# Order of the chunk pairs in one unit: pairs 0 to 7 in natural order, seven-product pairs at places 3, 5, 6 and 7

## The chip, the cores and the metric

The kernel runs on one core of one Trainium2 chip. The metric is device time in microseconds (us). Three runs of the kernel before gave a median of 2133.9 us (2133.49 to 2135.06). Engines are named as the profile names them: PE is TensorE (matmuls), PEld its weight loads, DVE is VectorE, ACT is ScalarE, POOL is GpSimd, and SP is SyncE, which here only issues DMAs.

## What is computed

The reference is one decoder layer on 16 meta tokens and 256 tokens, model width 2048, in float32: a feed-forward block, a mixer of attention and a short convolution, and a second feed-forward block. The change touches the second feed-forward block only:

```python
def swiglu_ffn(h, w_gu, w_down):
    gate, up = jnp.split(h @ w_gu, 2, axis=-1)
    return (jax.nn.silu(gate) * up) @ w_down

    s = s + merged @ w_out[layer]
    h = rms_norm(s, norm_ffn2[layer])
    s = s + 0.5 * swiglu_ffn(h, ffn2_w_gu[layer], ffn2_w_down[layer])
```

## The kernel before

**Precision.** Each float32 operand is split into a high part (a cast by ACT, `wh`, line 531) and a low part (a subtraction by DVE, `wl`, line 532). A product is three matmuls into one PSUM bank: high by high, low by high, high by low (lines 644 to 646).

**Units.** Feed-forward two has 5632 hidden columns, taken in eleven units of 512 columns of gate and 512 of up. A unit (`gate_up_mix`, line 763, through `mixed` and `linear_mix`) multiplies 256 tokens (two blocks of 128) by eight pairs of 128-row chunks of the weights. So each pair is a 2 x 2 block product, and it is done in one of three forms, which the plan of the unit gives by letter:

- D: eight products, straightforward, into banks 2, 3, 4 and x. Two weight tiles of two columns each.
- P: seven products, with sums of blocks in the place of blocks, into banks 1 to 7. Four weight tiles, the first with one column. The sums of the weight blocks were prepared earlier and lie in DRAM (`made`, list `MADE`, lines 74 and 75); they are loaded as `t24` and `t13` (lines 673 and 674). The sums of the activation blocks (`a.sums`) are computed in the kernel.
- S: as P, with the weight sums made on the spot by DVE. The first unit has none.

All pairs of a unit add up in the same eight banks. `left` (line 635) counts the products that each bank still lacks, and when a bank is complete, `done` in `mixed` evicts it. Bank x is fed by D pairs only, and its eviction is a copy by ACT to `u2x` (line 736). The pool has eight banks (line 88) for everything, transposes included.

**Order.** The plan of the first unit is `FFN2_FIRST` (line 49). Its first entry gives the form at each of the eight places, its last the pair that stands at each place: pairs 0, 1, 3, 4, 5, 2, 6, 7 as D, D, P, D, P, D, P, P. The other units have no such entry and take the pairs in order. `linear_mix` reads the list at line 632 and uses it for the weight loads (lines 666, 673, 674), the activation blocks (line 704) and their sums (line 711). Loads are called two places ahead (`far`); weight tiles are made up to three tiles ahead of their products (`step`, line 299, `AHEAD`). Buffers: three for `st`, two for `t24` (tag "tt"), four each for `wh` and `wl`.

**The activations of the first unit.** They come from the stage just before, the output projection `w_out` (`add_mix` with OUT_FIRST and OUT, lines 1263 and 1264), whose results lie token by token in `sT`. For each pair, `turned` (line 1174) transposes four blocks on PE into a bank (`h_ps`, line 1180) and splits them into high (`h`, ACT, line 1184) and low (DVE, line 1185). `sum_of_parts` (line 579) and `combine` (line 586) then make the block sums of a pair for P: one addition (`mf`, line 583), four short operations (`sums`, lines 589 to 592), and a split (`sp`, lines 614 and 615). `mf` and `sums` come from the tag "sc" with two buffers, the same two in which the one-column `wh` and `wl` of each P place are made (line 521).

Pairs 0 to 3 are transposed during the last part of the output projection, with the sums of pairs 2 and 3. For pairs 4 to 7, `out_done(1)` (line 1248) puts six jobs on the list `side`, and each place of the first unit takes one when its last product has been issued (line 660): the transposes of pair 4 at place 0, of pair 5 with its sum at place 1, of pair 6 with its sum at place 2, of pair 7 at place 3, the sum of pair 7 at place 4, and the norm (`norm_tok`) at place 5.

**Queues.** Each engine works off its queue in order. The order of a queue is fixed when the program is built, from the program's order and from when operands and buffers are expected to be free; so an instruction whose buffer isn't free can stand behind later ones.

Of the kernel before, what the change touches and what calls it, by code (L numbers as in the profile page):

```python
# [15 lines left out]
P = 128  # L16
# [4 lines left out]
F = 5632  # L21
DC = D // P
GC = 4
GW = GC * P
# [21 lines left out]
GATES = ("PSDSDSDS", (), {(0, 3): 1, (2, 1): 3, (4, 1): 5, (6, 1): 7}, ())  # L46
Q = ("DSDSDSDS", (), {(0, 1): 1, (2, 1): 3, (4, 1): 5, (6, 1): 7}, ())
B_PLAN = ("DSDSDSDS", (2, 4), {(0, 1): 1, (2, 1): 3, (4, 1): 5, (6, 1): 7}, ())
FFN2_FIRST = ("DDPDPDPP", (1,), {}, (), (0, 1, 3, 4, 5, 2, 6, 7))
FFN2 = ("DDPPDSPP", (1,), {(4, 1): 5}, ())  # L50
FFN2_MORE = ("DPPPDSPP", (2,), {(4, 1): 5}, ())
OUT_FIRST = ("DDSDSDSD", (1,), {(1, 1): 2, (3, 1): 4, (5, 1): 6}, ())
# [9 lines left out]
MORE_IN = (4, 5, 6, 7, 8, 9, 10)  # L62


def _made_in(plan):
    return [plan[4][i] if plan[4:] else i for i, kind in enumerate(plan[0]) if kind == "P"]


def _unit_plan(u):
    return FFN2_MORE if u in MORE_IN else FFN2 if u else FFN2_FIRST  # L70


GATE_UNITS = [GATES_FIRST] + [GATES] * (D // GW - 1)
MADE = [(0, d, p) for d, plan in enumerate(GATE_UNITS) for p in _made_in(plan)]
MADE += [(1, u, p) for u in range(F // GW) for p in _made_in(_unit_plan(u))]


@with_exitstack
def decoder_layer(ctx: ExitStack, tc: tile.TileContext, t, out):
    nc = tc.nc  # L80
# [9 lines left out]
    def bank(name):  # L90
        return psum.tile([P, 512], F32, tag="acc", name=name)
# [41 lines left out]
    def load_vectors():  # L133
# [7 lines left out]
        out=mask[:, T - P :],  # L141
        in_=mask[:, T - P :],
# [156 lines left out]
    def step(use, ring=True):  # L299

        ahead.append((use, ring))
        while sum(r for _, r in ahead) > AHEAD:
            ahead.pop(0)[0]()
# [10 lines left out]
    made = [[{} for _ in range(n // GW)] for n in (D, F)]  # L314
# [25 lines left out]

    for n, (f, u, p) in enumerate(MADE):
        spare.extend(Making(n, made[f][u], p, k) for k in range(2))
# [98 lines left out]
    def flush():  # L441
        while pending:
            pending.pop(0)()
# [74 lines left out]
    def parts(src, n=2, held=False):  # L518

        wh, wl = (  # L520
            tmp.tile([P, 1, GW], F32R, tag="sc", name=nm) if n == 1
            else (held_tile(nm) if held else wpool.tile([P, 2, GW], F32R, tag=nm, name=nm))
            for nm in ("wh", "wl")
        )
        wh, wl = wh[:, :n, :], wl[:, :n, :]
        with ExitStack() as order:
            if n == 1 and part_last:

                for ins in part_last:
                    order.enter_context(tc.issue_after(ins))  # L530
            part_last[:] = [nc.scalar.copy(out=wh, in_=src).ins]  # L531
            part_last.append(nc.vector.tensor_sub(wl, src, wh.bitcast(F32)).ins)  # L532
        return wh, wl
# [88 lines left out]
    def linear_mix(plan, a, w, name, done, k0=0, made=None, pairwise=False):  # L622

        kinds, turn_at, sums_at, by_load = plan[:4]
        at = plan[4] if plan[4:] else range(len(kinds))
        nd = kinds.count("D")
        ns = len(kinds) - nd
        left = {k: 2 * nd * (k in "234x") + ns * (k != "x") for k in "1234567x"}
        ps = {}

        def product(k, left_op, wh, wl):
            first = k not in ps
            if first:  # L640
                ps[k] = bank(name + k)
            left[k] -= 1
            hi, lo = left_op
            nc.tensor.matmul(ps[k], hi, wh, start=first, stop=False)  # L644
            nc.tensor.matmul(ps[k], lo, wh, start=False, stop=False)  # L645
            nc.tensor.matmul(ps[k], hi, wl, start=False, stop=left[k] == 0)  # L646
            if left[k] == 0:
                done(k, ps[k])

        def use(p, n, products):  # L650

            for k, left_op, wh, wl in products:
                product(k, left_op, wh, wl)
            if p in turn_at and later:
                later.pop(0)()
            if n == (1 if kinds[p] == "D" else 3):
                if p == 0:
                    flush()
                if side:
                    side.pop(0)()  # L660

        def load(p):

            st = wpool.tile([P, 4, GW], F32, tag="st", bufs=ST_BUFS, name="st")
            n = 3 if p in by_load or kinds[p] == "P" else 4
            nc.sync.dma_start(out=st[:, :n, :], in_=w[k0 // 2 + at[p], :, :n, :])
            if kinds[p] == "P":
                if pairwise:
                    t13s[p] = wpool.tile([P, 2, GW], F32, tag="tt", bufs=2, name="t13")
                else:  # L670
                    t13s[p] = aux.tile([P, 2, GW], F32, tag="act", name="t13")
                t24s[p] = wpool.tile([P, 2, GW], F32, tag="tt", bufs=2, name="t24")
                nc.sync.dma_start(out=t24s[p], in_=made[at[p]][:, 2:4, :])
                nc.sync.dma_start(out=t13s[p], in_=made[at[p]][:, 0:2, :])
            if kinds[p] == "S":
                if not by_load and (made is None or pairwise):
                    t13s[p] = wpool.tile([P, 2, GW], F32, tag="tt", bufs=2, name="t13")
                elif p not in by_load:
                    t13s[p] = aux.tile([P, 2, GW], F32, tag="act", name="t13")
                t24s[p] = wpool.tile([P, 2, GW], F32, tag="tt", bufs=2, name="t24")  # L680
            return st

        def sums(k):
            st, t13, t24 = loaded[k], t13s[k], t24s[k]
            if k not in by_load:
                nc.vector.tensor_add(t13, st[:, 1:3, :], st[:, 3:4, :].to_broadcast([P, 2, GW]))
            nc.vector.tensor_add(t24[:, 0, :], t13[:, 0, :], st[:, 2, :])
            last_sum[:] = [nc.vector.tensor_add(t24[:, 1, :], t24[:, 0, :], st[:, 0, :]).ins]  # L688

        t13s, t24s = {}, {}  # L690

        def prefetch(p):
            t13 = t13s[p] = aux.tile([P, 2, GW], F32, tag="act", name="t13")
            nc.gpsimd.dma_start(out=t13, in_=w[k0 // 2 + p, :, 1:3, :])
            nc.gpsimd.dma_start(out=t13, in_=w[k0 // 2 + p, :, 3:5, :], accum_op=ALU.add)

        far = 2 if by_load or (made is not None and not pairwise) else 1
        loaded = {k: load(k) for k in range(far)}
        for p, kind in enumerate(kinds):
            for k in by_load:  # L700
                if k == p + 4 or (p == 0 and k < 4):
                    prefetch(k)
            st = loaded[p]
            (a11, a21), (a12, a22) = ([a.block(2 * at[p] + c, i) for i in range(2)] for c in range(2))
            if kind == "D":
                tiles = [
                    (st[:, 1 - c :: 2, :], (("2", a1, 0), ("3", a1, 1), ("4", a2, 0), ("x", a2, 1)))
                    for c, (a1, a2) in enumerate(((a11, a21), (a12, a22)))
                ]
            else:  # L710
                s1, s2, s3, s4 = a.sums[at[p]]
                tiles = [
                    (st[:, 2:3, :], (("3", s4, 0),)),
                    (st[:, 0:2, :], (("1", a11, 1), ("2", a12, 0))),
                    (t24s[p], (("6", s2, 0), ("4", a22, 1))),
                    (t13s[p], (("5", s1, 0), ("7", s3, 1))),
                ]
            for n, (src, products) in enumerate(tiles):
                if n == 1 and p + far < len(kinds):
                    loaded[p + far] = load(p + far)  # L720
                wh, wl = parts(src, src.shape[1])
                if (p, n) in sums_at:

                    with tc.issue_after(part_last[1]):
                        sums(sums_at[p, n])
                products = [(k, left_op, wh[:, j, :], wl[:, j, :]) for k, left_op, j in products]
                step(lambda p=p, n=n, products=products: use(p, n, products), src.shape[1] > 1)
# [388 lines left out]
    for d in range(D // GW):  # L1116
# [28 lines left out]
        if d < 2:  # L1145
            n = 3 * d
# [42 lines left out]
    def add_mix(plan, a, w, k0, u, by, adds, end):  # L1189
# [26 lines left out]
        def done(k, ps):  # L1216
# [18 lines left out]
            if all(n in ev for n in "1234567x"):  # L1235
                pending.append(finish_adds)

        linear_mix(plan, a, w[u], "pd", done, k0)

    def out_done(u):  # L1240
# [59 lines left out]
    for half in thirds:  # L1300
# [4 lines left out]
        if final:  # L1305
            for q in range(2):
                nc.gpsimd.dma_start(
                    out=gfin[q],
                    in_=t["norm_final"][q * W2 : (q + 1) * W2].rearrange("(o d) -> o d", o=1).to_broadcast([P, W2]),
# [76 lines left out]
def _laid_out(np, inputs):  # L1386
# [8 lines left out]
    for name in ("ffn1_w_gu", "ffn1_w_down"):  # L1395
# [15 lines left out]
            np.stack([_quarter(*ws[f], 2 * p * P, u * GW + k * GW // 2, GW // 2) for k in range(2)])  # L1411
            for f, u, p in MADE
        ]
# [8 lines left out]
def _quarter(w, far, r, c, n):  # L1422

    a, b = w[r : r + P], w[r + P : r + 2 * P]
    return _stacked([a[:, c : c + n], a[:, far + c : far + c + n], b[:, far + c : far + c + n], b[:, c : c + n]])
# [24 lines left out]
```

## Time and profile before

| | value |
|---|---|
| median of three runs | 2133.9 us |
| the profiled execution, whole | 2133.6 us |
| its span, first to last instruction | 2131.8 us |
| mean granted TensorE clock | 0.999 |
| DMA | 562.04 MB, mean 264 GB/s |
| first unit of feed-forward two, first matmul | 1434.99 us from the span's start |
| later units, from one unit's transposes (`mt_ps`) to the next (1757.23, 1797.68, 1838.15) | 40.45 and 40.47 us |

Times in the trace are counted from the span's start. A row of the timeline gives start, length, engine, line, operation, output and inputs, shape and count, and in brackets how long the engine stood idle before it and what released it. Matmuls are pipelined: a 512-column matmul is recorded as 0.39 us long, but the next starts before it ends, so the distance between starts is what it costs. Rows of the table by stretches give, for each engine, busy time and the number of instructions.

### The profile page before, as it was taken

What the parts mean: (1) busy time and instruction counts of PE and PEld (TensorE: products, weight loads), DVE (VectorE), ACT (ScalarE), POOL (GpSimd) and SP (SyncE); (2) the same over time, 40 slices, a digit from 0 to 9 for tenths busy, and PEclk for the clock granted to TensorE, in tenths of its full rate; (3) what the DMA queues carried; (4) which work ended last, traced back from release to release, by engine and by line L of the source; (5) the groups of instructions that cost most, each with busy time, mean ns of one, the idle gap of its engine ahead of it and who ended that gap; (6) DMA issues with size and microseconds to landing.
All of it is one profiled execution on the core that took longest, in us unless ns stands there. A gap on an engine that the chain in (4) does not pass through costs nothing.

```text
span 2131.8 us, 33535 instructions
## 1 busy us (share of the span) xinstructions
PE 2118.6 (99%) x13096; PEld 1910.3 (90%) x13096; DVE 1765.0 (83%) x2458; ACT 1138.7 (53%) x1447; POOL 152.0 (7%) x241
## 2 busy tenths in 40 slices
PE   9999999999999999999999999999999999999998
PEld 9999999999999998899998888887888888888887
DVE  8777776677767878967888889998999999998997
ACT  6433343344443455645546655557665567656765
POOL 0111111111111110000000000000000100000000
PEclk9999999999999999999999999999999999999999
DMA  8989999999899875544455665566875988769863
GB/s 305 340 310 339 344 331 331 334 331 331 328 331 338 302 293 193 182 166 151 144 187 199 212 231 179 208 215 231 289 274 191 284 323 316 247 222 325 320 232 138
DMA packets 107007, 562.04 MB, mean 264 GB/s; under 512 B 12512, under 2 KB 12896, under 8 KB 66144
## 3 DMA queue, kind: packets, MB, share of 16 engines
q1 hardware_dynamic: 72720, 440.73, 57.6%
q0 software_dynamic: 33696, 118.50, 16.1%
q8 instruction: 102, 1.67, 0.3%
q10 hardware_dynamic: 432, 0.67, 0.1%
q14 instruction: 57, 0.47, 0.1%
HBM read 496.94 MB, written 58.72 MB: 261 GB/s over the span
## 4 chain that ended last, share of the span: by engine, by line
PE 99%; ACT 0%; DMA 0%; DVE 0%; issue 0%; SPq 0%; ACTq 0%
PE pg L644 6%; PE pg L645 6%; PE pg L646 6%; PE pd L427 4%; PE pd L425 4%; PE pu L425 4%; PE pu L426 4%; PE pu L427 4%; PE pd L426 4%; PE pg L425 4%; PE pg L427 4%; PE pg L426 4%; PE pd L644 4%; PE pd L646 4%; PE pd L645 4%; PE g L644 2%
## 5 line engine op out<-in xcount | busy, mean ns | idle before, releaser
L409 ACT CAST wh<-st 128x1024 fp32r<-128x1024 f32 x320 | 335.1, 1049 | 475.7 <-PE pu L426 143.2
L414 DVE TENSOR_TENSOR wl<-st,wh 128x1024 fp32r<-128x1024 f32 x320 | 390.3, 1223 | 217.9 <-ACT wh L409 217.7
L532 DVE TENSOR_TENSOR wl<-st,wh 128x1024 fp32r<-128x1024 f32 (+1 forms) x424 | 454.3, 1089 | 32.9 <-ACT wh L531 29.2
L531 ACT CAST wh<-st 128x1024 fp32r<-128x1024 f32 (+1 forms) x424 | 386.4, 945 | 153.6 <-PE pdx L645 27.7
L531 ACT CAST wh<-t 128x1024 fp32r<-128x1024 f32 x208 | 214.6, 1052 | 244.5 <-DVE t L688 184.0
L532 DVE TENSOR_TENSOR wl<-t,wh 128x1024 fp32r<-128x1024 f32 x208 | 248.2, 1221 | 58.8 <-ACT wh L531 54.4
L427 PE MATMUL pd<-mh,wl 128*128 128x272 f32 x704 | 203.1, 288 | 0.0
L425 PE MATMUL pg<-h,wh 128*128 128x272 f32 x704 | 201.9, 287 | 0.4 <-ACT wh L409 0.4
L425 PE MATMUL pd<-mh,wh 128*128 128x272 f32 x704 | 202.2, 287 | 0.0
L425 PE MATMUL pu<-h,wh 128*128 128x272 f32 x704 | 201.9, 287 | 0.0
L427 PE MATMUL pu<-h,wl 128*128 128x272 f32 x704 | 201.7, 287 | 0.0
L426 PE MATMUL pu<-h,wh 128*128 128x272 f32 x704 | 201.7, 286 | 0.0
L426 PE MATMUL pg<-h,wh 128*128 128x272 f32 x704 | 201.6, 287 | 0.0
L427 PE MATMUL pg<-h,wl 128*128 128x272 f32 x704 | 200.9, 287 | 0.0
L426 PE MATMUL pd<-ml,wh 128*128 128x272 f32 x704 | 200.8, 285 | 0.0
L645 PE MATMUL pg<-wh,h 128*128 128x512 f32 x373 | 146.1, 392 | 0.0
L644 PE MATMUL pg<-wh,h 128*128 128x512 f32 x373 | 145.5, 391 | 0.6 <-ACT h L1184 0.6
L646 PE MATMUL pg<-wl,h 128*128 128x512 f32 x373 | 145.4, 391 | 0.6 <-DVE wl L532 0.6
L426 PEld LDWEIGHTS pd<-ml,wh 128*128 128x128 f32 x704 | 133.5, 190 | 0.0
L425 PEld LDWEIGHTS pg<-h,wh 128*128 128x128 f32 x704 | 132.9, 189 | 0.7 <-ACT wh L409 0.7
L426 PEld LDWEIGHTS pg<-h,wh 128*128 128x128 f32 x704 | 132.8, 189 | 0.0
L426 PEld LDWEIGHTS pu<-h,wh 128*128 128x128 f32 x704 | 132.6, 188 | 0.0
(392 smaller groups left out, 5040.0 us busy)
## 6 DMA issues: line engine op xcount, KB each, us to landing
st<-in_ffn_w_gu_dram SPq DMA_DIRECT2D x121, 1024.0 KB, 7.4
st<-in_ffn_w_down_dram SPq DMA_DIRECT2D x82, 1024.0 KB, 7.1
mk<-in_ffn_made_of_dram POOLq DMA_DIRECT2D x108, 512.0 KB, 8.6
made<-mk POOLq DMA_DIRECT2D x108, 512.0 KB, 6.7
t<-made SPq DMA_DIRECT2D x108, 512.0 KB, 5.7
st<-in_ffn_w_gu_dram SPq DMA_DIRECT2D x51, 768.0 KB, 5.8
st<-in_w_in_dram SPq DMA_DIRECT2D x32, 1024.0 KB, 4.8
st<-in_w_gate_dram SPq DMA_DIRECT2D x29, 1024.0 KB, 4.8
```

Source lines behind the costliest of these rows:

```text
L409: nc.scalar.copy(out=wh[:, :m, :], in_=sw)
L414: last_wl[:] = [nc.vector.tensor_sub(wl[:, :m, :], sw, wh[:, :m, :].bitcast(F32)).ins]
L425: nc.tensor.matmul(a, wh[:, i, f], act.part(c, 0, t0, t1), start=first, stop=False)
L426: nc.tensor.matmul(a, wh[:, i, f], act.part(c, 1, t0, t1), start=False, stop=False)
L427: nc.tensor.matmul(a, wl[:, i, f], act.part(c, 0, t0, t1), start=False, stop=last)
L531: part_last[:] = [nc.scalar.copy(out=wh, in_=src).ins]
L532: part_last.append(nc.vector.tensor_sub(wl, src, wh.bitcast(F32)).ins)
L644: nc.tensor.matmul(ps[k], hi, wh, start=first, stop=False)
L645: nc.tensor.matmul(ps[k], lo, wh, start=False, stop=False)
L646: nc.tensor.matmul(ps[k], hi, wl, start=False, stop=left[k] == 0)
```

## The change

The list of pairs and its uses are removed, so the first unit takes pairs 0 to 7 in natural order, and the forms become D, D, D, P, D, P, P, P. Pairs 3, 5, 6 and 7 are P and 0, 1, 2 and 4 are D, before and after. Pair 2 moves from place 5 to place 2, and pairs 3, 4 and 5 each move one place back. The jobs on `side` keep their places.

```diff
-FFN2_FIRST = ("DDPDPDPP", (1,), {}, (), (0, 1, 3, 4, 5, 2, 6, 7))
+FFN2_FIRST = ("DDDPDPPP", (1,), {}, ())
...
-def _made_in(plan):
-    return [plan[4][i] if plan[4:] else i for i, kind in enumerate(plan[0]) if kind == "P"]
...
-MADE = [(0, d, p) for d, plan in enumerate(GATE_UNITS) for p in _made_in(plan)]
-MADE += [(1, u, p) for u in range(F // GW) for p in _made_in(_unit_plan(u))]
+MADE = [(0, d, p) for d, plan in enumerate(GATE_UNITS) for p, kind in enumerate(plan[0]) if kind == "P"]
+MADE += [(1, u, p) for u in range(F // GW) for p, kind in enumerate(_unit_plan(u)[0]) if kind == "P"]
...
-        kinds, turn_at, sums_at, by_load = plan[:4]
-        at = plan[4] if plan[4:] else range(len(kinds))
+        kinds, turn_at, sums_at, by_load = plan
...
-            nc.sync.dma_start(out=st[:, :n, :], in_=w[k0 // 2 + at[p], :, :n, :])
+            nc.sync.dma_start(out=st[:, :n, :], in_=w[k0 // 2 + p, :, :n, :])
...
-                nc.sync.dma_start(out=t24s[p], in_=made[at[p]][:, 2:4, :])
-                nc.sync.dma_start(out=t13s[p], in_=made[at[p]][:, 0:2, :])
+                nc.sync.dma_start(out=t24s[p], in_=made[p][:, 2:4, :])
+                nc.sync.dma_start(out=t13s[p], in_=made[p][:, 0:2, :])
...
-            (a11, a21), (a12, a22) = ([a.block(2 * at[p] + c, i) for i in range(2)] for c in range(2))
+            (a11, a21), (a12, a22) = ([a.block(2 * p + c, i) for i in range(2)] for c in range(2))
...
-                s1, s2, s3, s4 = a.sums[at[p]]
+                s1, s2, s3, s4 = a.sums[p]
```

## Prediction

> **What bounds the kernel now.** I read the page first: TensorE (PE) is busy for nearly the whole span, so a change in the order of one unit can gain only where PE waits inside that unit.
>
> ```profile
> PE 2118.6 (99%) x13096; PEld 1910.3 (90%) x13096; DVE 1765.0 (83%) x2458; ACT 1138.7 (53%) x1447; POOL 152.0 (7%) x241
> ```
>
> Next the chain of waits and PE's timeline around the unit. Its first matmul starts at 1434.99 us. Places 0 to 5 run until the last matmul of place 5, at 1467.78; by 1486.03 the unit's own products are done. The table by stretches sets these two stretches beside a later, steady one (us and length; then for PE, PEld, DVE, ACT, POOL busy us and count; clock; DMA share; GB/s):
>
> ```profile
> core 0: us, PE busy (x) PEld busy (x) DVE busy (x) ACT busy (x) POOL busy (x), PEclk, DMA share, GB/s
> 1434.98:1467.77 32.79, 32.79 (x146) 26.21 (x145) 28.14 (x41) 22.14 (x32) 0.00 (x0) 1.00 0.79 279
> 1467.77:1486.02 18.25, 15.57 (x64) 10.36 (x63) 14.78 (x26) 13.03 (x18) 0.00 (x0) 1.00 0.51 170
> 1757.00:1797.50 40.50, 40.50 (x184) 33.37 (x182) 38.87 (x44) 29.02 (x36) 0.00 (x0) 1.00 0.86 305
> ```
>
> The second stretch is the loose one: 64 PE instructions in 18.25 us, against 184 in 40.50. The timeline of that stretch, cut to the chain that matters:
>
> ```profile
> 1462.56 0.39 PE L644 MATMUL pg<-wh,h 128*128 128x512 f32 x1
> ...
> 1467.78 0.39 PE L646 MATMUL pgx<-wl,h 128*128 128x512 f32 x1
> ...
> 1468.92 0.58 ACT L736 COPY u2x<-pgx 128x512 f32<-128x512 f32 x1
> 1469.05 1.23 DVE L532 TENSOR_TENSOR wl<-st,wh 128x1024 fp32r<-128x1024 f32 x1 [1.49 <-ACT wh L531]
> ...
> 1469.56 0.66 PE L1180 MATMUL h_ps<-ident,sT 128*128 128x128 f32 x4 [1.39 <-ACT u2x L736]
> ...
> 1470.76 0.48 DVE L1185 SCALAR_TENSOR_TENSOR h<-h_ps,vec,h 128x256 fp32r<-128x256 f32 x1 [0.48 <-ACT h L1184]
> ...
> 1472.30 0.69 DVE L583 TENSOR_TENSOR mf<-h 128x512 f32<-128x512 f32 x1
> ...
> 1472.41 0.63 PE L1180 MATMUL h_ps<-ident,sT 128*128 128x128 f32 x4
> ...
> 1473.03 0.29 DVE L589 TENSOR_TENSOR sums<-mf 128x128 f32<-128x128 f32 x1
> ...
> 1475.67 0.69 DVE L615 TENSOR_TENSOR sp<-sums,sp 128x512 fp32r<-128x512 f32 x1
> ...
> 1476.66 0.68 DVE L532 TENSOR_TENSOR wl<-st,wh 128x512 fp32r<-128x512 f32 x1
> ...
> 1477.45 0.69 DVE L583 TENSOR_TENSOR mf<-h 128x512 f32<-128x512 f32 x1
> ...
> 1483.12 0.69 DVE L615 TENSOR_TENSOR sp<-sums,sp 128x512 fp32r<-128x512 f32 x1
> ...
> 1483.91 0.69 DVE L532 TENSOR_TENSOR wl<-st,wh 128x512 fp32r<-128x512 f32 x1
> ...
> 1486.03 0.40 PE L644 MATMUL pgx<-wh,h 128*128 128x512 f32 x1
> ```
>
> What the reader should see: the program asks for the transposes of pair 6 behind place 2 and those of pair 7 behind place 3, but they run at 1469.56 and 1472.41, behind place 5. They wait for the copy of bank "x" (u2x). The code has eight PSUM banks; a D place fills 2, 3, 4 and x, and the first P place opens 1, 6, 5 and 7. From then on all eight are held until x is complete, and x is complete with the last D place. Here that is place 5. Everything that pairs 6 and 7 need then comes in one string: transposes, split, block sums, and, since sums and the one-column weight tile of a P place share a tag with two buffers ("sc"), sum, weight tile, sum, weight tile one behind the other until 1483.91 + 0.69 = 1484.60.
>
> **What the stall is worth.** Place 5 (24 matmuls) starts at 1462.56 and its last matmul at 1467.78: 23 pitches in 5.22 us, 0.227 us each. In the loose stretch the groups of instructions count:
>
> ```profile
> L645 PE MATMUL pg<-wh,h 128*128 128x512 f32 x10 | 4.2, 423 | 0.0
> ...
> L645 PE MATMUL pg<-wh,sp 128*128 128x512 f32 x8 | 2.9, 397 | 0.0
> ...
> L1180 PE MATMUL h_ps<-ident,sT 128*128 128x128 f32 x8 | 1.3, 283 | 1.4 <-ACT u2x L736 1.4
> ...
> L646 PE MATMUL pgx<-wl,h 128*128 128x512 f32 x1 | 0.4, 388 | 0.0
> ```
>
> That is 10 + 8 = 18 products of three matmuls (14 of places 6 and 7, so four of unit 1 already), the last matmul of place 5, and 8 transposes. 55 x 0.227 = 12.49 us, and 18.25 - 12.49 = 5.76. The eight transposes cost PE between 0.55 (steady stretch: 40.50 - 176 x 0.227) and 1.69 (first stretch: four D places of 24 and two P places of 21 less that one matmul are 137; 32.79 - 137 x 0.227, small waits included). So PE loses 4.1 to 5.2 us here; I take 4.7, about the middle.
>
> The Trainium skill (Perfetto Trace Analysis, Identifying the Most-Contended Engine) says that matmul busy time is a poor measure of headroom and that weight-load busy time should be read in its place. The rows agree: 15.57 of 18.25 us looks like a loss of 2.7, while by weight loads (10.36 of 18.25 against 33.37 of 40.50) it would be 18.25 x (1 - 0.568/0.824) = 5.7 us, an estimate by that page; with it in place of 4.7 the sum below would end 1.0 us lower.
>
> **The change part by part.** The order of pairs goes from 0, 1, 3, 4, 5, 2, 6, 7 with P at places 2, 4, 6, 7 to 0 to 7 with P at 3, 5, 6, 7. In both, pairs 3, 5, 6 and 7 are P, so the list of prepared tiles, every load's size, and all 180 matmuls (4 x 24 + 4 x 21) stay. Instructions removed or added: none, 0 us. Only order moves:
>
> 1. The last D place is now 4, so x is complete one P place earlier: 21 x 0.227 = 4.8 us of PE work (place 5, pair 5, whose sums don't hang on x) now lies behind the transposes that need it. And place 2 is D: when it ends only four banks hold products, so the transposes of pair 6 can run there, 24 + 21 matmuls (10.2 us) before x is complete. Only pair 7 is left to wait for x.
>
> 2. Pair 6's string starts at place 2's end and place 6 comes 21 + 24 + 21 matmuls, 15 us, later. The price of such a string under load is that of pair 5 in this trace:
>
> ```profile
> 1446.59 0.60 PE L1180 MATMUL h_ps<-ident,sT 128*128 128x128 f32 x4
> ...
> 1451.36 0.48 DVE L1185 SCALAR_TENSOR_TENSOR h<-h_ps,vec,h 128x256 fp32r<-128x256 f32 x1
> 1451.62 0.39 PE L646 MATMUL pg<-wl,h 128*128 128x512 f32 x1
> 1451.87 0.69 DVE L583 TENSOR_TENSOR mf<-h 128x512 f32<-128x512 f32 x1
> 1451.99 0.47 PE L644 MATMUL pg<-wh,sp 128*128 128x512 f32 x1
> ...
> 1457.04 0.69 DVE L615 TENSOR_TENSOR sp<-sums,sp 128x512 fp32r<-128x512 f32 x1
> ...
> 1457.83 0.69 DVE L532 TENSOR_TENSOR wl<-st,wh 128x512 fp32r<-128x512 f32 x1
> ```
>
> From transposes to the sums' low part 11.1 us (1457.73 - 1446.59); unloaded, pair 6 took 6.8 (1476.36 - 1469.56). Both are under 15: hidden. The bank that these transposes borrow is the eighth that place 3 wants for its last product; in this trace the same happened one place earlier, and that product waited for 1451.84 and lost 1451.99 - 1451.62 - 0.23 = 0.14 us. It moves, it isn't added: 0.
>
> 3. Pair 7's string. Call X the end of place 4's last matmul. From the rows: x is copied and the transposes start 1.4 us behind X (1469.56 - 1468.17); then 6.8 to 11.1 us to the sums; then the one-column tile of place 6, which in program order takes its "sc" buffers behind this sum, 1.0 (1477.34 - 1476.36); its product, 3 x 0.227 = 0.7; then place 7's tile, a cast and a subtraction of about 0.7 each, 1.4, and its product, 0.7. Total 12.0 to 16.3 behind X. PE has from X places 5, 6 and 7: 63 x 0.227 = 14.3, and the four products of unit 1 that it took early here too, 2.7: 17.0. So the string fits with 0.7 to 5 us to spare, if the other products of a place go ahead of the late one, as they did here. Cost 0 to 2.0 (if pair 7's transposes are queued a few matmuls late); I take 0.5.
>
> 4. PE's queue: the transposes sit in PE's own order, and if x's copy is late everything behind them stands, as in the 1.39 us above. Here three matmuls or more of place 5 can stand ahead of them. Cost 0 to 1.4; I take 0.4, one-product-behind the lower end of (1.39 - 0.68 = 0.7) and nothing.
>
> 5. DVE. A P place costs it 3 x 1.23 + 0.68 = 4.4 us beside 4.8 of PE, a D place 2.5 beside 5.4. Now three P places end the unit instead of two. The unit's DVE work is 28.14 + 14.78 = 42.9 us; the shortened unit is 51.04 - 4.7 = 46.3 us, 93%, while the steady stretch runs at 38.87 of 40.50, 96%, with PE never idle. Cost 0 to 1.5; I take 0.2.
>
> 6. DMA. The three queued loads of each P place (0.75 + 2 x 0.5 MB) move as a block one place later, except those of pairs 6 and 7, which stay. SP issues pair 2's load ahead of those of pairs 3, 4 and 5. The first stretch runs at 279 GB/s and the steady one, with three P places in a row, at 305 without a PE wait: 0, and up to about 1 if a prepared tile comes late.
>
> Sum: -4.7 + 0.5 + 0.4 + 0.2 = -3.6 us. The profiled execution took 2133.6 us (2131.8 of span), so 2130.0; the median of the runs shown is 2133.9, so 2130.3.
>
> **Rivals.**
>
> *Full recovery.* The stall is at the upper end and nothing takes its place: -5.2, or 2128.7; some of the first stretch's small waits may go as well, to 2128.2. For it: no steady unit with three P places in a row waits. Against: pair 7 still hangs on x.
>
> *The stall only moves.* Pair 7's string takes its long form, place 6's tile is stuck behind the sum in "sc", and the queue order, fixed when the program is built, puts late products ahead of ready ones. Then 2.0 + 1.4 + 1.5 = 4.9 comes back: 2133.9 + 0.2 = 2134.1. For it: 1457.83 and 1477.45 show tile and sum handing these buffers to each other. Against: the 17.0 us of cover.
>
> *Slower: DVE falls behind in places 3 to 7.* Four P places and a D place are 4 x 4.4 + 2.5 = 20.1 us of DVE; three sums (0.69 + 4 x 0.29 + 0.69 = 2.5 each) and two splits (2 x 0.48 each) add 9.4, two serial waits between ACT and DVE at each split about 2 in all, first evictions 1.4: 32.9 against (84 + 24) x 0.227 = 24.5 of PE. If DVE enters place 3 without a lead, PE waits 8.4 in place of 4.7: +3.7, 2137.6. It decides when pair 5's and pair 6's sums both fall behind the start of place 3. Against: places 0 to 2 are now D, 7.4 us of DVE beside 16.3 of PE. The clock stays at 1.00 through the present stall, whose longest single wait is 1.39 us. The Trainium skill (TensorE: Matmul & The Clock Gate, HAM oscillation) has PE's clock halved after an idle gap over about 3.4 us; by that page one such gap would add some 1.7 us more, an estimate, and no row here has a gap that long.
>
> *It doesn't do what it says.* Queues are filled by readiness, not by program order alone, so the transposes of pair 6 may still be placed late. Then place 5's shift alone acts: two strings with 14.3 us of cover, about half of the gain, 2132; this lies within the forecast's spread.
>
> **How the numbers follow.** Forecast (with the last rival's half gain) 0.56, own range 2129.2 to 2132.5; full recovery 0.22; the stall moves 0.14; slower 0.08. What can be told from no change is about 0.2%, 4.3 us: below 2129.6 or above 2138.2. Faster takes full recovery and a few hundredths of the forecast's low edge: 0.25. Slower takes the part of the last case that passes 4.3 us: 0.07. The rest, 0.68, is within. The range reaches from 2128.2 to 2136.0: it holds all but the DVE case.
>
> **What would show it.** Right: in the changed profile the transposes of pair 6 run behind place 2, those of pair 7 behind place 4, PE's table for the unit shows about 47.4 us for the same 192 matmuls (137 + 55), and DVE stays under 96%. Wrong: transposes of pair 6 behind place 4 as well; a PE wait of over 1 us on "wl" or "sp" in places 6 and 7; ACT waiting for a prepared tile's DMA there; or time gained or lost outside 1430 to 1530 us, since nothing else is touched.

## The result, and the profile after

The changed kernel takes 2130.74 us (median of 12 runs, 2129.55 to 2134.48); the kernel before, in runs beside it, 2134.57 us (12 runs). The ratio is 0.9984 with a 95% interval of 0.9977 to 0.9992: 3.4 us faster, by the interval 1.7 to 4.9. The forecast was 3.6 us faster, 2130.3 us. The measured gain, 0.16%, is below the 0.2% that the prediction names as what can be told from no change.

The engines' busy times hardly change, as the first lines of the page of the changed kernel show:

```profile
span 2128.9 us, 33537 instructions
...
PE 2117.1 (99%) x13096; PEld 1910.4 (90%) x13096; DVE 1765.0 (83%) x2458; ACT 1138.9 (53%) x1447; POOL 152.2 (7%) x241
```

Same instruction counts on every computing engine: only order has changed. The table by stretches of the changed kernel (columns as in the prediction), places 0 to 5 up to about 1468 and what follows:

```profile
1435.30:1468.08 32.78, 32.72 (x150) 26.15 (x150) 29.25 (x48) 23.78 (x37) 0.00 (x0) 1.00 0.66 232
1468.08:1483.00 14.92, 14.33 (x64) 11.52 (x63) 14.41 (x22) 10.24 (x13) 0.00 (x0) 1.00 0.81 281
```

Both second stretches hold 64 PE instructions, 18.25 us long before and 14.92 now; but before, eight of them were transposes, and now none is. Weight loads fill 77% of it (11.52 of 14.92) in place of 57%. Like for like, the unit's first 192 matmuls with their 16 transposes take 47.12 us (1435.34 to 1482.46), where they took 51.04; the prediction named about 47.4. Over the unit DVE is busy 43.66 of 47.70 us, 92%.

To compare kernels I use one length throughout: from the first gate matmul of the unit to the first of the transposes (`mt_ps`) that run in unit 3, the first unit being unit 0. Between these two rows lie the same 572 matmuls and 32 transposes in every kernel here; the absolute position of the unit plays no part. First the timeline rows of the kernel before, then those of the changed one:

```profile
1434.99 0.39 PE L644 MATMUL pg<-wh,h 128*128 128x512 f32 x1
...
1574.08 0.27 PE L783 MATMUL mt_ps<-ident,cup 128*128 128x128 f32 x1
```

```profile
1435.34 0.39 PE L639 MATMUL pg<-wh,h 128*128 128x512 f32 x1
...
1452.93 0.60 PE L1175 MATMUL h_ps<-ident,sT 128*128 128x128 f32 x4
...
1463.60 0.39 PE L641 MATMUL pgx<-wl,h 128*128 128x512 f32 x1
...
1465.84 0.58 ACT L731 COPY u2x<-pgx 128x512 f32<-128x512 f32 x1
...
1466.08 0.69 DVE L611 TENSOR_TENSOR sp<-sums,sp 128x512 fp32r<-128x512 f32 x1
...
1466.56 0.60 PE L1175 MATMUL h_ps<-ident,sT 128*128 128x128 f32 x4
...
1469.10 0.39 PE L641 MATMUL pg<-wl,sp 128*128 128x512 f32 x1
...
1471.71 0.68 DVE L579 TENSOR_TENSOR mf<-h 128x512 f32<-128x512 f32 x1
...
1476.13 0.39 PE L640 MATMUL pg<-wh,h 128*128 128x512 f32 x1
...
1477.09 0.69 DVE L611 TENSOR_TENSOR sp<-sums,sp 128x512 fp32r<-128x512 f32 x1 [0.47 <-ACT sp L610]
...
1477.11 1.20 PE L639 MATMUL pg<-wh,sp 128*128 128x512 f32 x4 [0.59 <-ACT sp L610]
...
1478.30 1.82 DVE L528 TENSOR_TENSOR wl<-st,wh 128x512 fp32r<-128x512 f32 x2
...
1481.36 0.68 DVE L528 TENSOR_TENSOR wl<-st,wh 128x512 fp32r<-128x512 f32 x1
...
1482.46 0.39 PE L640 MATMUL pg<-wh,h 128*128 128x512 f32 x1
...
1570.95 0.27 PE L778 MATMUL mt_ps<-ident,cup 128*128 128x128 f32 x1
```

Before 139.09 us, after 135.61: 3.48 us shorter, which agrees with the measured gain. (The spans differ by 2.9; the unit itself starts 0.35 later in this execution, see the last section.) In the rows the reader can follow the forecast step by step. The transposes of pair 6 run at 1452.93, behind place 2, where they had run at 1469.56. Those of pair 7 wait for x, whose last matmul is at 1463.60, and run at 1466.56; no bracket stands behind that row, so no wait of PE is recorded there: products of place 5 stood ahead of them in its queue. ACT was late with the copy (done at 1466.42, 2.4 us behind the end of x's last matmul at 1463.99), and that was covered. Pair 7's string then ends with the sums at 1477.78, and PE stands still once, 0.59 us, for their high part. Place 6's one-column tile comes behind that sum, at 1478.30 (the row takes in a two-column tile that follows it), and place 7's at 1481.36. That place 6's tile stood behind pair 7's sum because of the two shared buffers is what own_after tests: there its cast runs at 1470.31, ahead of the sum, where it runs at 1476.95 here.

### The profile page after: what moved, and what is told of

It is laid out like the page before. It is cut to its first block, busy times and chain, and to the rows that moved or that the text cites. A ratio compares the mean times of both kernels' runs of the same rounds, so it can differ in the third digit from the quotient of the medians.

```text
span 2128.9 us, 33537 instructions
## 1 busy us (share of the span) xinstructions
PE 2117.1 (99%) x13096; PEld 1910.4 (90%) x13096; DVE 1765.0 (83%) x2458; ACT 1138.9 (53%) x1447; POOL 152.2 (7%) x241
## 4 chain that ended last, share of the span: by engine, by line
PE 98%; DMA 1%; ACT 1%; DVE 0%; issue 0%; SPq 0%; ACTq 0%
PE pg L641 6%; PE pg L639 6%; PE pg L640 6%; PE pd L423 4%; PE pd L421 4%; PE pu L421 4%; PE pu L422 4%; PE pu L423 4%; PE pd L422 4%; PE pg L423 4%; PE pg L421 4%; PE pg L422 4%; PE pd L639 4%; PE pd L641 3%; PE pd L640 3%; PE g L639 2%
```

## The experiments

The theory from the prediction: the eight banks are all held from the first P place until x is complete, so transposes that have not run by then wait, and the string behind them is longer than the work that covers it. The rivals: the order of pairs and loads itself; the place of x alone; the two buffers that sums and one-column tiles share; DVE's load. Twelve kernels tell them apart. In the table, "length" is the length defined above, "loss" is what it exceeds the shortest one by (133.67 us, in which no wait of PE is recorded), and the median and the ratio are against the kernel before in the same session. Gains in microseconds worked out from a ratio carry an interval of about 2 us to either side; the length is the finer measure. Each length is from one execution: the part from the unit's 241st matmul on, which no edit touches, takes 76.25 to 76.51 us in the fourteen kernels, so a difference of up to 0.3 us says nothing.

| kernel | length us | loss us | median us (before) | ratio, 95% interval |
|---|---|---|---|---|
| before | 139.09 | 5.42 | | |
| after | 135.61 | 1.94 | 2130.74 (2134.57) | 0.9984 [0.9977, 0.9992] |
| control | 138.87 | 5.20 | 2134.01 (2134.13) | 1.0 [0.9991, 1.0009] |
| pair6_early | 135.36 | 1.69 | 2130.09 (2134.13) | 0.9981 [0.9972, 0.999] |
| x_early | 139.59 | 5.92 | 2134.54 (2134.13) | 1.0001 [0.9993, 1.001] |
| early_transposes | 133.67 | 0 | 2128.43 (2134.13) | 0.9973 [0.9963, 0.9983] |
| d_first | 135.41 | 1.74 | 2131.06 (2134.42) | 0.9985 [0.9976, 0.9994] |
| after_early7 | 135.15 | 1.48 | 2129.46 (2134.42) | 0.9976 [0.9967, 0.9985] |
| own_before | 138.47 | 4.80 | 2134.38 (2134.42) | 1.0001 [0.9992, 1.001] |
| own_after | 134.35 | 0.68 | 2129.21 (2134.42) | 0.9976 [0.9967, 0.9985] |
| job6_early | 134.19 | 0.52 | 2129.61 (2134.21) | 0.9978 [0.9969, 0.9987] |
| job7_early | 138.53 | 4.86 | 2133.74 (2134.21) | 0.9998 [0.9989, 1.0007] |
| after_all_early | 135.08 | 1.41 | 2130.12 (2134.21) | 0.9979 [0.997, 0.9988] |
| x_early_own | 135.84 | 2.17 | 2131.53 (2134.21) | 0.9988 [0.9979, 0.9997] |

### control: another order, x and the first P place as before

```diff
-FFN2_FIRST = ("DDPDPDPP", (1,), {}, (), (0, 1, 3, 4, 5, 2, 6, 7))
+FFN2_FIRST = ("DDPPDDPP", (1,), {}, (), (0, 1, 3, 5, 2, 4, 6, 7))
```

> Order 0, 1, 3, 5, 2, 4, 6, 7 with forms D, D, P, P, D, D, P, P: other places for pairs 2, 4 and 5 and other load order than before, but the first P place is still 2 and the last D place still 5, so bank x is complete as late as before. Theory (bank x sets when the transposes of pairs 6 and 7 run): both still run behind place 5, PE loses 4 to 5.5 us there, time within 1 us of before. Rival (the order of the loads, or pair 2 standing in the way, made the difference): 1.5 to 3.5 us faster than before.

Loss 5.20 where before loses 5.42, time the same. The transposes stand still at the same point, as PE's timeline of this kernel shows:

```profile
1469.73 0.66 PE L1180 MATMUL h_ps<-ident,sT 128*128 128x128 f32 x4 [1.40 <-ACT u2x L736]
```

Three pairs and their loads are elsewhere and nothing is gained: another order that leaves x and the first P place where they were is worth nothing.

### pair6_early and x_early: one half of the change each

```diff
-FFN2_FIRST = ("DDPDPDPP", (1,), {}, (), (0, 1, 3, 4, 5, 2, 6, 7))
+FFN2_FIRST = ("DDDPPDPP", (1,), {}, (), (0, 1, 2, 3, 5, 4, 6, 7))
```

> Order 0, 1, 2, 3, 5, 4, 6, 7 with forms D, D, D, P, P, D, P, P: place 2 is D as in the changed kernel, so the transposes of pair 6 can run behind it, but the last D place is 5, so x is complete as late as before. Theory: only pair 7's string hangs on x, 10.3 to 14.6 us long, with 9.5 us of matmuls of places 6 and 7 and up to 2.7 of the next unit beside it: PE loses 0 to 2.5, 2 to 4 us faster than before. Rival (only the place at which x is complete matters): no gain, PE still loses over 4 us.

```diff
-FFN2_FIRST = ("DDPDPDPP", (1,), {}, (), (0, 1, 3, 4, 5, 2, 6, 7))
+FFN2_FIRST = ("DDPDDPPP", (1,), {}, (), (0, 1, 3, 2, 4, 5, 6, 7))
```

> Order 0, 1, 3, 2, 4, 5, 6, 7 with forms D, D, P, D, D, P, P, P: the last D place is 4 as in the changed kernel, but the first P place is 2, so the transposes of pairs 6 and 7 both wait for x. Theory: two sums and three one-column tiles stand in one string of 19 to 24 us behind place 4, with 17.0 us of cover: PE loses 2 to 7 us, 0 to 2.3 us faster than before. Rival (only the place at which x is complete matters): as the changed kernel, 3 to 4 us faster.

pair6_early gains all of it, 3.73 us of length, though x is complete as late as before; x_early gains nothing (loss 5.92, within the 2 to 7 expected, and 0.5 above before's), though x is complete as early as in the changed kernel. PE's timeline of pair6_early: pair 6's transposes behind place 2, pair 7's behind place 5 without a wait, and one short wait at the end:

```profile
1452.87 0.60 PE L1180 MATMUL h_ps<-ident,sT 128*128 128x128 f32 x4
...
1467.87 0.60 PE L1180 MATMUL h_ps<-ident,sT 128*128 128x128 f32 x4
...
1477.89 1.19 PE L644 MATMUL pg<-wh,sp 128*128 128x512 f32 x4 [0.73 <-ACT sp L614]
```

The timeline of x_early shows the other half's fate. Pair 6's string begins at 1465.14 and pair 7's at 1469.59, when pair 6's split (DVE, L1185) has released it; then sum of pair 6 (mf), one-column tile of place 5 (wl), sum of pair 7 (mf, sp), tiles of places 6 and 7, one behind the other until 1482.76, with PE idle for 2.50 us in one piece:

```profile
1465.14 0.63 PE L1180 MATMUL h_ps<-ident,sT 128*128 128x128 f32 x4
...
1469.59 0.63 PE L1180 MATMUL h_ps<-ident,sT 128*128 128x128 f32 x4 [0.16 <-DVE h L1185]
...
1470.49 0.68 DVE L583 TENSOR_TENSOR mf<-h 128x512 f32<-128x512 f32 x1
...
1475.06 0.68 DVE L532 TENSOR_TENSOR wl<-st,wh 128x512 fp32r<-128x512 f32 x1
...
1476.79 0.68 DVE L583 TENSOR_TENSOR mf<-h 128x512 f32<-128x512 f32 x1
...
1479.28 0.69 DVE L615 TENSOR_TENSOR sp<-sums,sp 128x512 fp32r<-128x512 f32 x1 [0.68 <-ACT sp L614]
1479.30 1.19 PE L644 MATMUL pg<-wh,sp 128*128 128x512 f32 x4 [2.50 <-ACT sp L614]
1480.08 0.69 DVE L532 TENSOR_TENSOR wl<-st,wh 128x512 fp32r<-128x512 f32 x1
...
1482.08 0.68 DVE L532 TENSOR_TENSOR wl<-st,wh 128x512 fp32r<-128x512 f32 x1
```

Not all of the 5.92 is waiting. The table by stretches of x_early shows PE's granted clock at 0.50 for 3.4 us, soon after that wait of 2.50 us:

```profile
1475.00:1480.80 5.80, 3.31 (x14) 2.38 (x14) 4.84 (x10) 3.13 (x4) 0.00 (x0) 1.00 0.87 285
1480.80:1484.20 3.40, 3.40 (x9) 2.63 (x8) 2.25 (x4) 2.05 (x3) 0.00 (x0) 0.50 0.92 331
1484.20:1490.00 5.80, 5.80 (x27) 4.81 (x26) 5.80 (x8) 4.00 (x6) 0.00 (x0) 1.00 0.90 315
```

Eight matmuls start there 0.43 us apart in place of 0.227, which makes 1.6 us. Without it the loss would be 4.3, about 1 us less than before's: by itself the earlier end of x saves about that much waiting, and the slower clock takes it back. So the half of the change that counts is the D place at 2, not the earlier end of x.

### early_transposes, job6_early, job7_early: the jobs alone, in the order of before

```diff
-                        lambda: [turned(4), squares(0, 1, 0), squares(1, 1, 0)],
-                        lambda: [turned(5), hn.sum_of_parts(5)],
-                        lambda: [turned(6), squares(0, 1, 1), hn.sum_of_parts(6)],
-                        lambda: [turned(7), squares(1, 1, 1)],
+                        lambda: [turned(4), turned(5), squares(0, 1, 0), squares(1, 1, 0)],
+                        lambda: [turned(6), turned(7), squares(0, 1, 1), squares(1, 1, 1), hn.sum_of_parts(5)],
+                        lambda: hn.sum_of_parts(6),
+                        lambda: None,
                         lambda: hn.sum_of_parts(7),
```

> Order and forms of before; only the side jobs move: transposes of pairs 4 and 5 at place 0, of 6 and 7 at place 1, the sums of 5, 6, 7 at places 1, 2 and 4. All transposes run while four banks are free. Theory: the wait for x is gone without any change of order, PE loses under 1.2 us where it lost 4.7, 3 to 4.5 us faster than before. Rival (order of pairs, loads or DVE's load in the unit): less than 1 us faster.

```diff
-                        lambda: [turned(5), hn.sum_of_parts(5)],
-                        lambda: [turned(6), squares(0, 1, 1), hn.sum_of_parts(6)],
+                        lambda: [turned(5), turned(6), hn.sum_of_parts(5)],
+                        lambda: [squares(0, 1, 1), hn.sum_of_parts(6)],
```

> Order and forms of before; of the side jobs only the transposes of pair 6 move, from place 2 to place 1, so they run while banks are free and only pair 7's wait for x behind place 5. Theory as it now stands (two pairs waiting for x make one string that is too long, one pair's string is covered): PE loses 1 to 2.5 us over the floor, 3 to 4.5 us faster than before, as with pair 2 at place 2. Rival (the changed order itself brings part of the gain): less than 2 us faster.

```diff
-                        lambda: [turned(5), hn.sum_of_parts(5)],
+                        lambda: [turned(5), turned(7), hn.sum_of_parts(5)],
...
-                        lambda: [turned(7), squares(1, 1, 1)],
+                        lambda: squares(1, 1, 1),
```

> Order and forms of before; of the side jobs only the transposes of pair 7 move, from place 3 to place 1, so only pair 6's wait for x behind place 5. Its sum stands ahead of pair 6's tile, pair 7's sum and pair 7's tile in the two shared buffers. Theory (the string of sums and tiles counts, and pair 6 heads it): nearly the whole string is left, 0 to 2 us faster than before. Rival (the number of transposes behind x counts, whichever pair): as with pair 6's moved, 3 to 4.5 us faster.

early_transposes is the shortest of all and the fastest kernel here, 2128.43 us; its gain is larger than I expected (5.42 us of length against 3 to 4.5). PE's timeline of it has all sixteen transposes before the first P product, and no row with a bracket up to the end of the length:

```profile
1434.99 0.39 PE L644 MATMUL pg<-wh,h 128*128 128x512 f32 x1
...
1440.43 0.38 PE L1180 MATMUL h_ps<-ident,sT 128*128 128x128 f32 x2
...
1440.89 0.82 PE L1180 MATMUL h_ps<-ident,sT 128*128 128x128 f32 x6
...
1446.80 1.04 PE L1180 MATMUL h_ps<-ident,sT 128*128 128x128 f32 x8
...
1568.66 0.27 PE L783 MATMUL mt_ps<-ident,cup 128*128 128x128 f32 x1
```

That shows that the wait for x, with the string behind it, was the stall: order, forms and loads are those of before. It is 1.94 us of length shorter than the changed kernel; their times, from two sessions, have overlapping intervals.

Moving one pair's transposes separates the two again. With pair 6's early (job6_early) 0.52 us of loss is left, less than the 1 to 2.5 that I expected of pair 7's string. With pair 7's early (job7_early) 4.86 is left: the number of transposes behind x is the same, but the string starts with pair 6's sum. (Pair 6's sums are also used one P place earlier than pair 7's, which is 21 x 0.227 = 4.8 us less PE work beside them; these two reasons aren't separated here.) The first wait of job7_early is that of before, in PE's timeline:

```profile
1469.52 0.66 PE L1180 MATMUL h_ps<-ident,sT 128*128 128x128 f32 x4 [1.39 <-ACT u2x L736]
...
1479.68 0.50 PE L644 MATMUL pg<-wh,h 128*128 128x512 f32 x1 [1.18 <-ACT wh L531]
```

### own_before, own_after, x_early_own: buffers of their own for the sums

In the kernel before, the changed kernel and x_early alike; four tiles of the pool of activations stand free at this time:

```diff
-            f = tmp.tile([P, 2, SEQ], F32, tag="sc", name="mf")
+            own = self is own_of[0] and p in (5, 6, 7)
+            f = (apool if own else tmp).tile([P, 2, SEQ], F32, tag="act" if own else "sc", name="mf")
...
-            q = tmp.tile([P, 4, P], F32, tag="sc", name="sums")
+            q = (apool if own else tmp).tile([P, 4, P], F32, tag="act" if own else "sc", name="sums")
...
-    hn = Mixed(h3, G_FFN2, False)
+    hn = own_of[0] = Mixed(h3, G_FFN2, False)
```

> The kernel before, with the sums of pairs 5, 6 and 7 in buffers of their own (from the pool of activations, where four stand free) in place of the two that they share with the one-column weight tiles. Theory (the bank is the cause, the shared buffers only lengthen the string): the transposes still run behind place 5, PE loses 3 to 4.5 us, 0.3 to 1.7 us faster than before. Rival (the shared buffers are the cause): PE loses under 1.5 us, over 3 us faster.

> The changed kernel, with the sums of pairs 5, 6 and 7 in buffers of their own in place of the two that they share with the one-column weight tiles. Theory: what is left at place 6 (0.87 us) is partly place 6's tile standing behind pair 7's sum: 0.3 to 0.7 us faster than the changed kernel. Rival (it is pair 7's transposes alone): no difference of 0.2 us or more in the stall.

> The order 0, 1, 3, 2, 4, 5, 6, 7 with x complete at place 4 and the transposes of pairs 6 and 7 both behind it, and now the sums of pairs 5, 6 and 7 in buffers of their own. Theory (there the loss is the string of sums and one-column tiles in the two shared buffers): PE loses under 2.5 us over the floor in place of 5.9, 3 to 5 us faster than before. Rival (the loss comes from two pairs' transposes behind one bank): under 1.5 us faster than before.

In before, own buffers leave a loss of 4.80 of 5.42 (3 to 4.5 expected): the wait for x comes first, and the time is the same. In the changed kernel they take 1.26 of the 1.94 that was left (more than the 0.3 to 0.7 expected), and in x_early 3.75 of 5.92, of which 1.6 is the slower clock that now stays away. So the shared buffers are a second cause, which only counts once the transposes are on time or x is early. PE's timeline of x_early_own has this where x_early had 2.50 us:

```profile
1480.44 1.19 PE L647 MATMUL pg<-wh,sp 128*128 128x512 f32 x4 [0.31 <-ACT sp L617]
```

Its time (0.9988, 2.6 us, by the interval 0.6 to 4.5, where I expected 3 to 5) agrees with its length (3.25 us shorter) within the interval.

### d_first, after_early7, after_all_early: better versions, and DVE's load

```diff
-FFN2_FIRST = ("DDPDPDPP", (1,), {}, (), (0, 1, 3, 4, 5, 2, 6, 7))
+FFN2_FIRST = ("DDDDPPPP", (1,), {}, (), (0, 1, 2, 4, 3, 5, 6, 7))
```

> Order 0, 1, 2, 4, 3, 5, 6, 7 with forms D, D, D, D, P, P, P, P: x is complete at place 3 and only four banks are held until then, so no transposes wait for a bank, but four P places stand in a row with the sums of pairs 6 and 7 beside them. Theory (bank): PE loses under 1.2 us, 3 to 4.5 us faster than before. Rival (DVE falls behind in rows of P places: 4 x 4.4 us of copies and two sums against 19.1 us of PE): PE loses 3 to 8 us, no faster than before or up to 3 us slower.

```diff
-                        lambda: [turned(6), squares(0, 1, 1), hn.sum_of_parts(6)],
-                        lambda: [turned(7), squares(1, 1, 1)],
+                        lambda: [turned(6), turned(7), squares(0, 1, 1), hn.sum_of_parts(6)],
+                        lambda: squares(1, 1, 1),
```

> The changed kernel with the transposes of pair 7 moved from place 3 to place 2, beside those of pair 6, where banks are free. Theory: the rest of the stall, 0.87 us at the end of place 6, goes too: 0.5 to 1.0 us faster than the changed kernel, 3.9 to 4.4 faster than before. Rival (what is left is DVE's or the shared buffers' doing): PE still loses 0.7 us or more at place 6, the same time as the changed kernel.

after_all_early has in the changed kernel the jobs of early_transposes.

> The changed kernel with all transposes early: pairs 4 and 5 at place 0, 6 and 7 at place 1. Theory (once no transposes wait for a bank the order of pairs is worth nothing): the unit is as short as with the order of before and the same jobs, 5 to 6 us faster than before. Rival (the natural order with its three P places in a row has a cost of its own): PE still loses 0.5 us or more, 4 to 5 us faster.

d_first, with four P places in a row, loses 1.74: not the 3 to 8 of the DVE rival, though more than the 1.2 of mine. Its one wait in PE's timeline is for the cast of a one-column tile by ACT:

```profile
1478.99 0.50 PE L644 MATMUL pg<-wh,sp 128*128 128x512 f32 x1 [1.30 <-ACT wh L531]
```

after_early7 comes 0.46 of length under the changed kernel, just short of what I expected, and a wait of 0.41 us for such a cast is left. From the unit's 138th matmul to its 193rd it takes 13.27 us (1468.84 to 1482.11), the changed kernel 13.36 (1469.10 to 1482.46): at the end of the unit the rival was right, and what is left there isn't pair 7's wait for x. after_all_early refutes a part of the theory: with no transposes behind x at all, the natural order still loses 1.41, where the order of before loses nothing. Its only recorded PE wait in the unit is small:

```profile
PE mt_ps L778 <- DVE cup L765: 0.3, 1, 0.3
```

That 0.3 us is at the eviction of the unit. Set beside early_transposes by parts, 0.69 us of the 1.41 is lost up to the 138th matmul (33.57 against 32.88 us), 0.17 from there to the 193rd (12.90 against 12.73) and 0.55 behind it, where the 0.3 lies. Of the first part, 0.27 is lost ahead of the second group of transposes, where both kernels still work on the first two pairs; the rest is gaps of about 0.1 us. With three P places at the end, sums and tiles are closer together; that this is the reason is only argued, and it doesn't fit the part lost early.

## Why the prediction was right, point by point

**The stall.** Taken at 4.7 us (bounds 4.1 to 5.2). The loss of 5.42 in the table takes in more than the stretch that this was worked out for, the one from the unit's 138th matmul to its 193rd: 1467.78 to 1486.03 in before, 18.25 us. In early_transposes the same 55 matmuls take 12.73 us without any transposes between them, as PE's timeline shows:

```profile
1467.87 0.39 PE L646 MATMUL pgx<-wl,h 128*128 128x512 f32 x1
...
1480.60 0.39 PE L644 MATMUL pg<-wh,h 128*128 128x512 f32 x1
```

The eight transposes that before has there cost 0.88: by the rows of early_transposes above, two take 0.38 and eight 1.04, so 0.11 for each. 18.25 - 12.73 - 0.88 = 4.64: the term was right. The other 0.78 of the 5.42 lies in places 0 to 5. The weight-load estimate by the Trainium skill (Perfetto Trace Analysis, Identifying the Most-Contended Engine), 5.7 us, came out about 1 us too high for this stretch; the 2.7 by matmul busy time was 1.9 too low.

**Step 1, where the gain comes from.** It named two things: x complete one P place earlier, and pair 6's transposes at place 2. The runs show that the first is worth about 1 us of waiting by itself, with nothing of it left in the time (x_early, loss 5.92, of which 1.6 is the slower clock), and isn't needed (pair6_early 1.69 beside 1.94 with both). The second alone carries the gain. Here the text was wrong to put the 4.8 us of cover first.

**Step 2** held: pair 6's string was hidden. It took 13.8 us (1452.93 to 1466.77), longer than the 11.1 of the long form and under the 15 of cover.

**Step 3, pair 7's string:** 0.5 taken, bounds 0 to 2.0. From the 138th matmul to the 193rd 0.63 us is left (13.36 - 12.73). The string started 2.6 us behind the end of x's last matmul, not 1.4, and took 11.2 us from transposes to sums (1477.78 - 1466.56), not 6.8 to 11.1. With these two the text's own sum is 17.6 us against 17.0 of cover, 0.6 short, which is the size measured. The shared buffers account for what is left: own_after takes 12.67 us there (1469.10 to 1481.77).

**Step 4, PE's queue,** 0.4 taken: no wait is recorded at these transposes. **Step 5, DVE,** 0.2 taken: DVE was busy 92% of the unit, under the 96% that I named as a sign of trouble, and 97% of the last stretch (14.41 of 14.92 us). The one wait recorded there is for ACT; how far DVE's tiles between the sums' operations lengthened the string isn't separated. **Step 6, DMA:** no PE wait on a load.

**The sum.** By parts: 4.64 - 0.63 = 4.01 us gained in the stretch; 0.10 lost ahead of it (33.76 us up to the 138th matmul with 16 transposes, against 32.78 with eight and 0.88 for eight more); 0.44 lost behind it (88.49 against 88.05 us), where the first transposes of unit 1 come. That makes -4.01 + 0.10 + 0.44 = -3.47, the -3.48 of the lengths, against -4.7 + 1.1 = -3.6. The forecast was right in mechanism and in size: the stall was 4.64 for 4.7, and 1.17 came back for 1.1. How the 1.1 is made up was in part luck: 0.6 of it was set down to PE's queue and to DVE, where no wait is recorded, and the 0.54 outside the stretch was not foreseen.

**The rivals.** Full recovery did not come with this change; it exists, by another edit (early_transposes). The stall moving is what happened to x_early, not here. The slower case named its own condition, pair 5's and pair 6's sums both behind the start of place 3, and that came true: in DVE's rows they begin at 1455.17 and 1460.23, and place 3's first product at 1453.28 in PE's. Its price of 8.4 us did not come, neither here nor in d_first with four P places in a row (loss 1.74). For the clock that rival names an idle gap of 3.4 us; the traces here show the halved clock after shorter ones (last section). That the transposes of pair 6 would still be placed late did not happen: 1452.93.

## What to carry to other kernels

When one engine waits for a buffer that is held by a long accumulation, ask first whether the waiting work could have been done before the accumulation opened its last buffers: moving three side jobs one or two places ahead gained more here than reordering the accumulation. Of several jobs that wait for one buffer, what counted here was which one waited, not how many: moving the one that is needed first brought 4.9 us, moving the other 0.6. And two small tags that share buffers put unrelated work in one line; such a line shows only once the longer wait ahead of it is gone.

## What was not expected

DVE at nearly full occupancy did no harm: in early_transposes it was busy 19.88 of 20.00 us while PE waited for nothing, as the table by stretches of that kernel shows:

```profile
1470.00:1490.00 20.00, 20.00 (x93) 16.17 (x92) 19.88 (x28) 15.21 (x18) 0.00 (x0) 1.00 0.77 275
```

The unit's start, set by all that comes before, varied by 2.4 us between executions (1434.92 in job7_early to 1437.32 in x_early_own) although nothing ahead of it was changed. In x_early_own the chain of waits begins with a first load that ends 1.1 us later than in before, 9.24 against 8.17 (first the row of before, then that of x_early_own). PE then waits 1.72 us, and from 12.08 to 15.49 us its granted clock is 0.50, where before has 1.00; by 30 us x_early_own is 2.4 us behind, and it stays so up to the unit. The table by stretches of x_early_own is the last fence below. So a profile's whole span is a poor measure of an edit of a few microseconds, and a length inside the trace a better one.

```profile
2.59 5.58 DMA mk<-in_ffn_w_gu_dram
```

```profile
2.59 6.65 DMA mk<-in_ffn_w_gu_dram
```

```profile
12.08:15.49 3.41, 3.41 (x18) 3.41 (x17) 3.31 (x7) 3.41 (x8) 0.00 (x0) 0.50 1.04 422
```

That is the same as in x_early. From 7 to 2120 us of the span, only two times in the fourteen traces does PE stand still for longer than 1.40 us, 2.50 in x_early and 1.72 in x_early_own, and only behind these two is the granted clock 0.50, for 3.41 us each, from about 1.5 and 1.7 us after the wait ends. Behind the waits of 1.30 to 1.40 us in before, control, d_first, own_before, job7_early and after_all_early it stays at 1.00. So a wait that is long enough costs a second time, 1.6 us in x_early; two cases don't give the threshold.
